# Two transformer blocks on one core: late row factors, the convolution on VectorE, and row-form projections with an earlier attention

## The chip, the cores and the metric

The kernel runs on one core of one Trainium2 chip, in one launch. The metric is the device time of that launch in microseconds (us), the median of several runs. The engines are called TensorE (PE in the profile; PEld is its weight load), VectorE (DVE), ScalarE (ACT), GpSimd (POOL) and SyncE (SP, which issues nearly all DMAs here).

## The reference

256 tokens of width 1024 in float32 pass through two blocks, one layer each.

```python
# first block
h = rmsnorm(x, norm1_g);  z = h @ w_in + b_in          # q k v c_a c_b g_a g_b
br_a = neighbourhood_attention(q, k, v, rpb) @ w_na_out
u = dwconv31(c_a * sigmoid(c_b))                       # 512 channels, 31 taps along the tokens
br_b = silu(layernorm(u)) @ w_conv_out
x = x + (sigmoid(g_a) * br_a + sigmoid(g_b) * br_b) @ w_out
up = dwconv3(rmsnorm(x, norm2_g) @ w_up)               # 2 x 2816 channels
x = x + (gelu(gate) * val) @ w_down                    # gate, val: the halves of up
x = rmsnorm(x, norm_f_g)
# second block
aq, ak, av, mq, mk, mv, mi, mf, mo, ga, gm = split(rmsnorm(x, norm1_gain) @ w_in_2)
att_b = sliding_window_attention(rope(rmsnorm(aq)), rope(rmsnorm(ak)), av, sinks) @ w_branch_attn
hm = rmsnorm(mlstm(mq, mk, mv, mi, mf)) * sigmoid(mo)
mixed = sigmoid(ga) * att_b + sigmoid(gm) * (hm @ w_branch_mlstm)
x = x + mixed @ w_out_2
x = x + peer_ffn(rmsnorm(x, norm2_gain))               # 16 of 16384 experts for each of 8 heads
```

## The kernel before

Every matmul is carried out in the reduced format fp32r as three products, so that it comes out near float32: an operand is split into a high part (rounded to fp32r) and a low part (the rest), and high by high, low by high and high by low are added up. Weights come in **granules** of 128 x 1024 (512 KB): `granule` (L199) has SP load one into one of four `raw` buffers, ScalarE copies out its high part `wh` (L214), and VectorE subtracts to get its low part `wl` (L215; GpSimd for the first two). There are three buffers for each part. A granule is used in one of two forms. `mm_cols` (L233) holds weights stationary and moves 256 columns, all the tokens: 24 matmuls a granule, output with channels on the partitions. `mm_rows` (L243) holds 128 tokens stationary and moves 512 columns of weights: 12 matmuls a granule, output with tokens on the partitions. `turn` (L315) transposes four squares of 128 x 128 into a bank of PSUM and splits them to get a column form. PSUM has four banks "mm" and four "at".

The emitted code says which instructions there are and who needs what; a scheduler sets each engine's order from it, and that order is then fixed. `drive` (L149) interleaves generators by weight: a stream of weight 4 gets four steps where one of weight 1 gets one.

**First block** (L327). The normalized rows are scaled by row factor and gain (`scaled_cols`, L296) and turned. `stream1` (L401) projects c_b and c_a of half the channels (`glu(2)`, which ends with the product `up`, L396), then q, k and v. `stream2` does `glu(0)` and the gates. Beside them run the convolution and the attention. Of the 31 taps of the convolution, half the channels are done on VectorE (L433, L441), half by a product on ScalarE (L445) and an addition on GpSimd (L446). `rows_out` (L653) is the output projection: it computes the new rows `xn`, their squares, the row factor (`power`, L272, on GpSimd), scales by factor and gain (L303) and turns the result for the FFN (L319). The FFN runs over 22 steps `f`: two granules up, the 3-tap convolution, GELU, one granule `down` into four accumulating banks. At its end the last rows are scaled and turned in the same way for the second block.

**Second block** (L725). `stream1` runs alone: akv, the gates' product (`wif`, L788), aq, mq, mk, mv. Then `drive` interleaves `stream2` (mo, ga2, gm2, in column form), the attention at weight 4 and the mLSTM at weight 2. The attention starts with `qk_norm` (L893): for each half i of the tokens ScalarE squares, VectorE sums, takes a reciprocal root by Newton steps (`rsqrt`, L257) and multiplies by factor and gains (L902, L904, L905), GpSimd rotates (L910 to L915, eight instructions), and TensorE transposes q and k (L922, L927, L929). The mLSTM starts with `gates` (L828), a long chain of small VectorE instructions on 8 partitions. The two branch projections ba and bm (column form), the output projection and the experts follow. The experts take the second half of the span and are not touched.

Of the kernel before, what the change touches and what calls it, by code (L numbers as in the profile page):

```python
# [51 lines left out]
def _col(v):  # L52
# [4 lines left out]
         ("cb", 4), ("lg", 4), ("lb", 4), ("fw", 132), ("fb", 44), ("mg", 8), ("gb", 1))  # L57
_ROWS = (("n1", D), ("n2", D), ("nf", D), ("m1", D), ("m2", D), ("b_v", 512), ("qg", 64), ("kg", 64),
# [20 lines left out]
def pack(inputs):  # L79
# [13 lines left out]
        _blocks_b(w2[:, 1792:2304]), _blocks_a(w2[:, 2304:3328], 512), _blocks_b(w2[:, 3344:4368]),  # L93
        _blocks_b(w2[:, 4368:5392]), _blocks_b(w2[:, 5392:6416]), _blocks_b(a["w_branch_attn_2"][0]),
        _blocks_b(a["w_branch_mlstm_2"][0]), _blocks_a(a["w_out_2"][0], 512),
# [16 lines left out]
        _col(a["ffn_dw_b"][0]), _col(a["ml_out_norm_gain_2"][0]), gb], axis=1)  # L112
    rows = np.concatenate([
        a["norm1_g"][0], a["norm2_g"][0], a["norm_f_g"], a["norm1_gain_2"][0], a["norm2_gain_2"][0],
        bi[1024:1536], a["q_norm_gain_2"][0], a["k_norm_gain_2"][0], a["attn_sinks_2"][0]])
# [33 lines left out]
def drive(*gens):  # L149

    live = [[0.0, w, g] for w, g in gens]
    while live:
        e = min(live, key=lambda s: s[0])
        try:
            step = next(e[2])
            e[0] += (step or 1.0) / e[1]
        except StopIteration:
            live.remove(e)


class Block:
# [71 lines left out]
    def mm_cols(self, out, w, x, nk, first=True, last=True, off=0):  # L233

        wh, wl = (t[:, off:off + nk * P].rearrange("p (k n) -> p k n", n=P) for t in w)
        xh, xl = x
        mm = self.nc.tensor.matmul
        for k in range(nk):
            mm(out, wh[:, k], xh[:, k], start=(first and k == 0), stop=False)  # L239
            mm(out, wh[:, k], xl[:, k], start=False, stop=False)  # L240
            mm(out, wl[:, k], xh[:, k], start=False, stop=(last and k == nk - 1))  # L241
# [63 lines left out]

    def warm(self, n):
# [20 lines left out]
def first_block(B, rp):  # L327
    tc, nc, A = B.tc, B.nc, B.A
    with ExitStack() as es:
# [71 lines left out]
        def stream1():  # L401
            yield from glu(2)
            for name, dst, bn in (("q", qT, "b_q"), ("k", kT, "b_k")):
                for n in range(0, 4, 2):
                    b = pair(name, n)
                    for j in range(2):
                        nc.vector.tensor_scalar(dst[:, n + j], b[:, j * T:(j + 1) * T], B.col(bn, n + j), None,
                                                op0=OP.add)
# [11 lines left out]
        def stream2():  # L420
            yield from glu(0)
# [8 lines left out]
        def taps(c0, engines):  # L430
            for c, e in enumerate(engines, c0):
                if e == "D":
                    nc.vector.tensor_scalar(y[:, c], up[:, c, 0:T], B.col("cw", 31 * c), B.col("cb", c), op0=OP.mult,  # L433
                                            op1=OP.add)
                else:
                    nc.scalar.activation(y[:, c], up[:, c, 0:T], AF.Identity, scale=B.col("cw", 31 * c),
                                         bias=B.col("cb", c))
            for k in range(1, 31):
                for c, e in enumerate(engines, c0):
                    if e == "D":  # L440
                        nc.vector.scalar_tensor_tensor(y[:, c], up[:, c, k:k + T], B.col("cw", 31 * c + k), y[:, c],  # L441
                                                       op0=OP.mult, op1=OP.add)
                    else:
                        t = pool.tile([P, T], F32, tag="tap", name="tap", bufs=16)
                        nc.scalar.activation(t, up[:, c, k:k + T], AF.Copy, scale=B.col("cw", 31 * c + k))  # L445
                        nc.gpsimd.tensor_tensor(y[:, c], y[:, c], t, op=OP.add)  # L446
                if k % 3 == 0:
                    yield

        def conv2():  # L450
            while "up2" not in state:
                yield 0.25
            yield from taps(2, "DP")

        def conv():
            while "up0" not in state:
                yield 0.25
            yield from taps(0, "DP")
# [36 lines left out]
        def attention():  # L495
            O = (pool.tile([P, 4, T], FR, name="oh"), pool.tile([P, 4, T], FR, name="ol"))
            for c in range(4):
# [3 lines left out]
                for par in range(2):  # L501
# [24 lines left out]
                    nc.vector.tensor_copy(t, pt.rearrange("p (k q) -> p k q", k=2))  # L526
# [13 lines left out]
        drive((1.0, stream1()), (0.7, conv2()))  # L540
# [4 lines left out]
        drive((1.0, stream2()), (1.3, conv()), (2.0, attention()))  # L545
# [21 lines left out]
        g2 = B.gain(rp, "n2", "gain")  # L567
        X = B.xcol()
        x1 = rows_out(B, rp, "wo", M, x0, 0.5, g2, X, pool,
                      ("qT", "kT", "v", "y", "th", "sig", "oh", "ol"))  # L570


    with ExitStack() as es:
# [3 lines left out]
        late = []  # L577
        acc = [B.bank("at") for _ in range(4)]
# [9 lines left out]

        for f in range(NFF):
            b = B.bank("mm")  # L590
            for j in range(2):
                B.mm_cols(b[:, j * T:(j + 1) * T], B.sec("ffn", 3 * f + j), X, 8)
            u = pool.tile([P, 2, T + 2], F32, tag="u", name="u", bufs=2)
            nc.gpsimd.memset(u[:, :, 0:T + 2:T + 1], 0.0)
            nc.scalar.activation(u[:, :, 1:T + 1], b.rearrange("p (a t) -> p a t", a=2), AF.Copy)
            c = pool.tile([P, 2, T], F32, tag="c", name="c", bufs=2)
            for j in range(2):
                ch = f + NFF * j
                w3 = [B.col("fw", 3 * ch + k) for k in range(3)]
                nc.scalar.activation(c[:, j], b[:, j * T:(j + 1) * T], AF.Identity, scale=w3[1], bias=B.col("fb", ch))  # L600
# [16 lines left out]
        g3 = B.gain(rp, "m1", "gain")  # L617
        gf = B.row_bcast(pool, "nf")
# [696 lines left out]
```

## Time and profile before

| | |
|---|---|
| time, median of 3 runs | 1455.04 us (1454.49 to 1455.75) |
| time of the profiled execution | 1454.76 us |
| its span, first to last instruction | 1453.0 us |
| mean granted TensorE clock | 0.997 |
| busy: TensorE, VectorE, ScalarE, GpSimd | 98%, 75%, 52%, 8% |
| bytes by DMA | 251.44 MB, mean 173 GB/s |

The span is that of one profiled execution; its own time is 1.76 us longer than its span. Busy shares are averages over stages with different limits. A time in a row is the start of an instruction in microseconds from the start of the span, followed by how long it took. A busy TensorE is not one at its peak: matmuls overlap, so their pace is read from one start to the next.

### The profile page before, as it was taken

The page shows a single profiled execution, that of the slowest core. Times are in us where ns is not written, and L with a number is a line of the kernel's source. Part 1 is how long each engine was busy: PE and PEld are TensorE (multiplying, and loading weights), DVE is VectorE, ACT ScalarE, POOL GpSimd, SP SyncE. Part 2 cuts the span into 40 slices and gives each one's busy share as a digit, 9 for nine tenths or more (in the row PEclk, how much of TensorE's full clock was granted, in tenths as well). Part 3 has the DMA queues.
Part 4 walks back from the last instruction along what each step waited for, and adds up shares of the span by engine and source line. Part 5 has one row for each costly group of instructions (what it writes and reads, how often), then busy time and mean ns, then how long its engine had stood idle before and what let it go on. Part 6 is the DMA issues. An engine that isn't in the chain of part 4 may idle for free.

```text
span 1453.0 us, 26393 instructions
## 1 busy us (share of the span) xinstructions
PE 1429.1 (98%) x10351; PEld 1297.6 (89%) x10351; DVE 1092.5 (75%) x1971; ACT 761.2 (52%) x1185; POOL 110.2 (8%) x157
## 2 busy tenths in 40 slices
PE   8899999999999999999999999999999999999998
PEld 7778989999888988988999999999998888888887
DVE  6988876777787567674997976877849999666665
ACT  7476656656564666554454444344444444445443
POOL 4543000000204000001000000000000000000000
PEclk9999999999999999999999999999999999999999
DMA  7534656666466433475455565555565555666663
GB/s 266 168 115 133 180 193 180 187 188 215 135 184 207 144 95 117 145 240 152 148 173 178 170 189 174 161 162 167 167 207 171 172 175 163 189 201 189 192 198 130
DMA packets 70110, 251.44 MB, mean 173 GB/s; under 512 B 8025, under 2 KB 8417, under 8 KB 69730
## 3 DMA queue, kind: packets, MB, share of 16 engines
q1 hardware_dynamic: 69698, 249.17, 55.0%
q8 instruction: 81, 1.33, 0.4%
q10 hardware_dynamic: 288, 0.59, 0.2%
q14 instruction: 43, 0.35, 0.1%
HBM read 247.63 MB, written 2.11 MB: 172 GB/s over the span
## 4 chain that ended last, share of the span: by engine, by line
PE 89%; DVE 7%; issue 1%; ACT 1%; DMA 1%; POOL 1%; SPq 0%; POOLq 0%; ACTq 0%
PE mm L239 16%; PE mm L240 16%; PE mm L241 16%; PE mm L1258 8%; PE mm L1260 8%; PE mm L1259 8%; PE at L1236 2%; PE mm L253 2%; DVE wl L215 2%; PE mm L254 2%; PE mm L252 2%; DVE y L441 2%; PE at L585 1%; PE at L586 1%; PE at L587 1%
## 5 line engine op out<-in xcount | busy, mean ns | idle before, releaser
L215 DVE TENSOR_TENSOR wl<-raw,wh 128x1024 fp32r<-128x1024 f32 x454 | 558.1, 1232 | 202.9 <-ACT wh L214 197.0
L214 ACT ACTIVATE wh<-raw 128x1024 fp32r<-128x1024 f32 (+1 forms) x457 | 479.9, 1052 | 405.6 <-PE mm L240 322.0
L241 PE MATMUL mm<-xh,wl 128*128 128x256 f32 x1952 | 556.3, 285 | 5.6 <-DVE wl L215 5.6
L239 PE MATMUL mm<-xh,wh 128*128 128x256 f32 x1952 | 559.7, 287 | 0.9 <-ACT xh L225 0.9
L240 PE MATMUL mm<-xl,wh 128*128 128x256 f32 x1952 | 557.0, 285 | 0.1
L241 PEld LDWEIGHTS mm<-xh,wl 128*128 128x128 f32 x1952 | 376.2, 193 | 8.7 <-DVE wl L215 6.8
L239 PEld LDWEIGHTS mm<-xh,wh 128*128 128x128 f32 x1952 | 376.0, 193 | 7.1 <-issue 2.9
L240 PEld LDWEIGHTS mm<-xl,wh 128*128 128x128 f32 x1952 | 376.4, 193 | 4.6 <-issue 3.3
L1258 PE MATMUL mm<-wh,wsh 128*128 128x512 f32 x512 | 201.8, 394 | 0.0
L1260 PE MATMUL mm<-wh,wsl 128*128 128x512 f32 x512 | 199.7, 390 | 0.0
L1259 PE MATMUL mm<-wl,wsh 128*128 128x512 f32 x512 | 199.4, 390 | 0.0
L225 ACT ACTIVATE wsh<-W 128x256 fp32r<-128x256 f32 x128 | 53.4, 418 | 188.9 <-PE mm L1259 188.5
L1260 PEld LDWEIGHTS mm<-wh,wsl 128*128 128x128 f32 x512 | 96.2, 188 | 20.3
L1259 PEld LDWEIGHTS mm<-wl,wsh 128*128 128x128 f32 x512 | 96.3, 188 | 19.2
L1258 PEld LDWEIGHTS mm<-wh,wsh 128*128 128x128 f32 x512 | 96.2, 188 | 18.9
L226 DVE TENSOR_TENSOR wsl<-W,wsh 128x256 fp32r<-128x256 f32 x128 | 54.1, 424 | 50.0 <-ACT wsh L225 49.9
L446 POOL TENSOR_TENSOR y<-y,tap 128x256 f32<-128x256 f32 x60 | 58.1, 969 | 52.3 <-ACT tap L445 48.3
L253 PE MATMUL mm<-wl,xh 128*128 128x512 f32 (+1 forms) x160 | 61.1, 382 | 0.6 <-DVE wl L215 0.6
L254 PE MATMUL mm<-wh,xl 128*128 128x512 f32 (+1 forms) x160 | 61.1, 382 | 0.2 <-DVE xl L226 0.2
L252 PE MATMUL mm<-wh,xh 128*128 128x512 f32 (+1 forms) x160 | 61.1, 382 | 0.0
L1239 DVE SCALAR_TENSOR_TENSOR W<-at,W 128x512 f32<-128x512 f32 x64 | 42.7, 686 | 22.5 <-PE at L1236 22.3
L1230 DVE TENSOR_TENSOR bh<-eq,parts 128x512 f16<-128x512 f16 x128 | 48.8, 418 | 0.0
(342 smaller groups left out, 1578.5 us busy)
## 6 DMA issues: line engine op xcount, KB each, us to landing
raw<-in_ws_dram SPq DMA_DIRECT2D x199, 512.0 KB, 3.6
raw<-in_pd_dram SPq DMA_DIRECT2D x128, 512.0 KB, 3.6
raw<-in_pu_dram SPq DMA_DIRECT2D x128, 512.0 KB, 3.6
bias<-in_rpb_dram SPq DMA_DIRECT2D x2, 1024.0 KB, 7.6
x<-in_x_dram SPq DMA_DIRECT2D x4, 256.0 KB, 3.5
r_m<-in_rows_dram SPq DMA_DIRECT2D x2, 512.0 KB, 3.7
mb<-negm_d SPq DMA_DIRECT2D x4, 256.0 KB, 5.1
x<-xn SPq DMA_DIRECT2D x2, 512.0 KB, 5.6
```

Source lines behind the costliest of these rows:

```text
L214: nc.scalar.activation(wh[:, c], raw[:, c], AF.Copy)
L215: eng.tensor_sub(wl[:, c], raw[:, c], wh[:, c].bitcast(F32))
L239: mm(out, wh[:, k], xh[:, k], start=(first and k == 0), stop=False)
L240: mm(out, wh[:, k], xl[:, k], start=False, stop=False)
L241: mm(out, wl[:, k], xh[:, k], start=False, stop=(last and k == nk - 1))
L252: mm(outs[i], xh[:, k0 + k, ts], wh[:, k], start=st, stop=False)
L253: mm(outs[i], xh[:, k0 + k, ts], wl[:, k], start=False, stop=False)
L254: mm(outs[i], xl[:, k0 + k, ts], wh[:, k], start=False, stop=en)
L446: nc.gpsimd.tensor_tensor(y[:, c], y[:, c], t, op=OP.add)
L1258: nc.tensor.matmul(a, wp[0][:, ts], u[0][:, ns], start=(i == 0), stop=False)
L1259: nc.tensor.matmul(a, wp[0][:, ts], u[1][:, ns], start=False, stop=False)
L1260: nc.tensor.matmul(a, wp[1][:, ts], u[0][:, ns], start=False, stop=(i == NE - 1))
```

## The change

It has four parts. (1) At two steps, the entry of the FFN and the entry of the second block, rows are no longer multiplied by their factor before they are turned: only the gain is applied (`plain_cols`), and the factor is applied to the product, on rows as a per-partition scale and on columns by a factor that is spread over the partitions with two small matmuls (`across`). The FFN's input has a buffer of its own, and the first three f's do the first half of K before the second. (2) All taps of the convolution run on VectorE, two channel groups at a time; copies of q, k and the attention weights go to ScalarE; both `glu` come first. (3) In the second block mo, ga2, gm2, ba and bm are done by rows, and the mixed rows are turned afterwards. (4) The second block's `stream1` ends after aq; mq, mk and mv go to `stream2`, so that attention and mLSTM (weights 1.9 and 1.5) are interleaved with them.

```diff
+    def plain_cols(self, pool, src, g, x, k0, i, width=512):
+        for c in range(0, 512, width):
+            ns = slice(k0 * P + c, k0 * P + c + width)
+            y = pool.tile([P, width], F32, tag="nrm", name="nrm", bufs=4)
+            self.nc.vector.tensor_tensor(y, src[:, ns], g[:, ns], op=OP.mult)
+            self.turn(y, x, k0 + c // P, width // P, i)
+
+    def across(self, pool, rp, r, tag):
+        w = rp.tile([P, 2, P], F32, tag="nrm", name="rw", bufs=4)
+        for i in range(2):
+            nc.vector.tensor_copy(w[:, i:i + 1], bc(r[i], P))
+        b = self.bank("at")
+        for i in range(2):
+            nc.tensor.matmul(b[:, i * P:(i + 1) * P], w[:, i], self.ident, start=True, stop=True)
+        rb = pool.tile([P, T], F32, tag=tag, name="rb")
+        nc.scalar.activation(rb, b[:, 0:T], AF.Copy, scale=32.0)
+        return rb
...
+        def taps(c0):
...
             for k in range(1, 31):
-                for c, e in enumerate(engines, c0):
...
+                for c in cs:
+                    nc.vector.scalar_tensor_tensor(y[:, c], up[:, c, k:k + T], B.col("cw", 31 * c + k), y[:, c],
+                                                   op0=OP.mult, op1=OP.add)
+                if k % 2 == 0:
                     yield
...
-        drive((1.0, stream1()), (0.7, conv2()))
+        cv = conv()
+        lead((1.0, stream1()), (1.6, cv))
...
-        drive((1.0, stream2()), (1.3, conv()), (2.0, attention()))
+        drive((1.0, stream2()), (2.0, cv), (1.8, attention()))
...
+        ups = {}
+        ahead = [B.sec("ffn", 3 * f) for f in range(3)]
+        for kh in range(2):
+            for f, w in enumerate(ahead):
+                if f not in ups:
+                    ups[f] = B.bank("mm")
+                B.mm_cols(ups[f][:, 0:T], w, X, 4, kh == 0, kh == 1, kh * 512, 4 * kh)
...
-            nc.scalar.activation(u[:, :, 1:T + 1], b.rearrange("p (a t) -> p a t", a=2), AF.Copy)
+            nc.vector.tensor_tensor(u[:, :, 1:T + 1], b.rearrange("p (a t) -> p a t", a=2), bc_at(rb, 1, 2),
+                                    op=OP.mult)
...
+    if late:
+        return out, r
...
+        def stream2():
             for name, dst in (("mq", mq), ("mk", mk)):
                 for n in range(0, 4, 2):
                     b = pair(name, n)
-                    nc.scalar.activation(dst[:, n:n + 2], b.rearrange("p (a t) -> p a t", a=2), AF.Copy)
+                    nc.vector.tensor_tensor(dst[:, n:n + 2], b.rearrange("p (a t) -> p a t", a=2),
+                                            bc_at(st["rb"], 1, 2), op=OP.mult)
                     yield
...
             for name, dst in (("mo", so), ("ga2", ta), ("gm2", tb)):
-                for n in range(0, 8, 2):
-                    b = pair(name, n)
...
+                for nh in range(2):
...
+                        B.mm_rows(bs, B.sec(name, 4 * nh + gi), X, 2 * gi, 2, 512, gi == 0, gi == 3)
...
-        drive((1.0, stream2()), (4.0, attention()), (2.0, mlstm()))
+        drive((1.0, stream2()), (1.9, attention()), (1.5, mlstm()))
...
+        def second(i, nh, ns, b):
+            t = tb[:, i, ns]
+            nc.vector.scalar_tensor_tensor(t, t, 1.0, b, op0=OP.add, op1=OP.mult)
+            nc.vector.tensor_tensor(t, t, pa[:, i, ns], op=OP.add)
+            B.turn(t, Y, 4 * nh, 4, i)
```

`lead` interleaves like `drive`, but returns when its first generator ends.

The scheduler's order of VectorE's instructions at the start of the convolution, before (`y` on L433 and L441 are the taps, L407 copies q, L396 is `up`):

```order
L396 SCALAR_TENSOR_TENSOR up<-mm,cols,sig 128x256 x2
L433 TENSOR_SCALAR y<-up,cols 128x256
L215 TENSOR_TENSOR wl<-raw,wh 128x1024
L441 SCALAR_TENSOR_TENSOR y<-up,cols,y 128x256 x6
L215 TENSOR_TENSOR wl<-raw,wh 128x1024
L407 TENSOR_SCALAR qT<-mm,cols 128x256 x2
L441 SCALAR_TENSOR_TENSOR y<-up,cols,y 128x256
L215 TENSOR_TENSOR wl<-raw,wh 128x1024
```

and now (taps on L474 and L478, low parts on L231, `up` on L435):

```order
L435 SCALAR_TENSOR_TENSOR up<-mm,cols,sig 128x256 x2
L474 TENSOR_SCALAR y<-up,cols 128x256 x2
L478 SCALAR_TENSOR_TENSOR y<-up,cols,y 128x256 x16
L432 TENSOR_SCALAR sig<-sig 128x512
L231 TENSOR_TENSOR wl<-raw,wh 128x1024 x2
L478 SCALAR_TENSOR_TENSOR y<-up,cols,y 128x256 x4
L231 TENSOR_TENSOR wl<-raw,wh 128x1024 x2
```

Eighteen taps now stand between `up` and the next low part, where one stood.

TensorE's order where q and k of the first half of the tokens are transposed (L922 to L929), before, in the midst of the projection mo:

```order
L240 MATMUL mm<-xl,wh 128x256
L241 MATMUL mm<-xh,wl 128x256
L922 MATMUL at<-ident,qk 128x128 x8
L927 MATMUL at<-ident,qk 128x128
L929 MATMUL at<-ident,ks 128x128
L239 MATMUL mm<-xh,wh 128x256
```

and now (L996 to L1003), after all of mq and four matmuls of mk; L255 to L257 are the three products of `mm_cols`, L958 transposes a row of the gates:

```order
L257 MATMUL mm<-xh,wl 128x256
L255 MATMUL mm<-xh,wh 128x256
L256 MATMUL mm<-xl,wh 128x256
L255 MATMUL mm<-xh,wh 128x256
L256 MATMUL mm<-xl,wh 128x256
L996 MATMUL at<-ident,qk 128x128 x8
L1001 MATMUL at<-ident,qk 128x128
L1003 MATMUL at<-ident,ks 128x128
L958 MATMUL at<-ident,fi 128x8 x2
```

Before, mq, mk, mv and two granules of mo came ahead of these transposes; now only mq and the start of mk do. The second half's transposes now stand 33 matmuls behind the transposes of `mt` (L958), two matmuls before the end of mk.

VectorE's order around the row that releases the rotation of the first half, before (L902 to L905 are the products of `qk_norm`, L267 and L268 Newton steps, L858 the gates' scan):

```order
L902 TENSOR_TENSOR qk<-qk,rsy 128x1152
L215 TENSOR_TENSOR wl<-raw,wh 128x1024
L904 TENSOR_TENSOR qk<-qk,qg 128x1024
L905 TENSOR_TENSOR qk<-qk,qg 128x128
L267 SCALAR_TENSOR_TENSOR rst<-rsy 128x18
L215 TENSOR_TENSOR wl<-raw,wh 128x1024
L268 TENSOR_TENSOR rst<-rst,ss 128x18
```

and now (L976 to L979; L874 takes mq out of PSUM and multiplies it by the spread factor):

```order
L976 TENSOR_TENSOR qk<-qk,rsy 128x1152
L932 COPY gz_4742<-gz 8x2x4
L974 TENSOR_SCALAR ss<-ss 128x18
L978 TENSOR_TENSOR qk<-qk,qg 128x1024
L979 TENSOR_TENSOR qk<-qk,qg 128x128
L874 TENSOR_TENSOR mq<-mm,rb 128x512
L931 TENSOR_TENSOR gz<-gz_4742 8x2x120
L932 COPY gz<-gz_4742 8x2x8
L280 TENSOR_SCALAR rsy<-ss 128x18
L231 TENSOR_TENSOR wl<-raw,wh 128x1024
```

The row of mq, which waits for the last matmul of mq, now stands between the release of the rotation and the next low parts.

## Rows read from the trace of the kernel before

Times are in us from the start of the span; a line of `...` marks rows left out.

**Rows 1.** The page, part 1: busy time, share of the span, instructions.

```profile
PE 1429.1 (98%) x10351; PEld 1297.6 (89%) x10351; DVE 1092.5 (75%) x1971; ACT 761.2 (52%) x1185; POOL 110.2 (8%) x157
```

**Rows 2.** Windows: window, its length, engines' busy us (instructions), PEclk, DMA share, GB/s.

```profile
50.00:75.00 25.00, 23.17 (x127) 20.24 (x128) 22.48 (x30) 8.12 (x9) 7.16 (x8) 0.93 0.56 174
200.00:225.00 25.00, 24.61 (x194) 24.07 (x195) 19.63 (x43) 19.05 (x32) 0.31 (x3) 1.00 0.43 138
425.00:450.00 25.00, 25.00 (x202) 24.64 (x201) 24.83 (x68) 14.06 (x20) 8.46 (x6) 1.00 0.55 179
650.00:675.00 25.00, 22.05 (x150) 20.42 (x149) 11.38 (x19) 9.15 (x16) 4.53 (x4) 0.93 0.50 160
```

**Rows 3.** TensorE's waits: engine, line, releaser, us in total, times, longest us.

```profile
PE mm L241 <- DVE wl L215: 5.6, 6, 2.0
...
PE mm L253 <- DVE wl L215: 0.6, 1, 0.6
```

**Rows 4.** TensorE's timeline: start, us, line, out<-in, form. Second block aq, transposes, experts' query.

```profile
415.16 0.39 PE L253 MATMUL mm<-wl,xh 128*128 128x512 f32 x1
...
417.88 0.39 PE L253 MATMUL mm<-wl,xh 128*128 128x512 f32 x1
...
475.71 1.03 PE L922 MATMUL at<-ident,qk 128*128 128x128 f32 x8
...
849.92 0.28 PE L239 MATMUL mm<-xh,wh 128*128 128x256 f32 x1
...
850.28 0.28 PE L239 MATMUL mm<-xh,wh 128*128 128x256 f32 x1
```

**Rows 5.** TensorE's timeline, single waits: in brackets the idle time before and its releaser.

```profile
46.01 0.39 PE L241 MATMUL mm<-xh,wl 128*128 128x256 f32 x1 [1.98 <-DVE wl L215]
...
51.18 0.39 PE L241 MATMUL mm<-xh,wl 128*128 128x256 f32 x1 [2.04 <-DVE wl L215]
...
199.48 0.44 PE L319 MATMUL at<-ident,nrm 128*128 128x128 f32 x2 [2.20 <-DVE nrm L303]
...
390.19 1.32 PE L319 MATMUL at<-ident,nrm 128*128 128x128 f32 x8 [0.76 <-DVE nrm L303]
...
396.25 0.44 PE L319 MATMUL at<-ident,nrm 128*128 128x128 f32 x2 [1.45 <-DVE nrm L303]
...
658.00 0.44 PE L319 MATMUL at<-ident,nrm 128*128 128x128 f32 x2 [2.37 <-DVE nrm L303]
```

**Rows 6.** VectorE's timeline, beside the convolution with GpSimd idle.

```profile
59.05 0.47 DVE L441 SCALAR_TENSOR_TENSOR y<-up,cols,y 128x256 f32<-128x256 f32 x1
59.44 0.86 DVE L407 TENSOR_SCALAR kT<-mm,cols 128x256 f32<-128x256 f32 x2
...
60.62 1.21 DVE L215 TENSOR_TENSOR wl<-raw,wh 128x1024 fp32r<-128x1024 f32 x1
```

**Rows 7.** Groups of VectorE's instructions from 25 to 130 us: busy us, mean ns, idle before.

```profile
L441 DVE SCALAR_TENSOR_TENSOR y<-up,cols,y 128x256 f32<-128x256 f32 x60 | 43.3, 721 | 1.3
L215 DVE TENSOR_TENSOR wl<-raw,wh 128x1024 fp32r<-128x1024 f32 x27 | 37.0, 1378 | 2.1 <-ACT wh L214 2.1
```

**Rows 8.** GpSimd's timeline, rotation of q and k, first and second half.

```profile
441.46 1.46 POOL L910 TENSOR_TENSOR rt<-qk,cos 128x144 f32<-128x144 f32 x1 [42.70 <-DVE rst L267]
...
443.36 4.44 POOL L910 TENSOR_TENSOR rt<-qk,cos 128x144 f32<-128x144 f32 x1
...
450.78 0.54 POOL L910 TENSOR_TENSOR rt<-qk,cos 128x144 f32<-128x144 f32 x1
...
457.46 0.24 POOL L915 COPY ks<-qk 128x64 f32<-128x64 f32 x1
```

**Rows 9.** TensorE's first matmul after the gates' product; VectorE's products with the gains.

```profile
403.33 0.40 PE L252 MATMUL mm<-wh,xh 128*128 128x512 f32 x1
...
441.04 0.27 DVE L905 TENSOR_TENSOR qk<-qk,qg 128x128 f32<-128x128 f32 x1
...
446.03 1.21 DVE L904 TENSOR_TENSOR qk<-qk,qg 128x1024 f32<-128x1024 f32 x1
```

More of the change, by code (lines that the diff above doesn't have):

```diff
@@ L157, in drive, with lead @@
         except StopIteration:
+            live.remove(e)
+def lead(main, *others):
+    live = [[0.0, w, g] for w, g in (main,) + others]
+    first = live[0]
+    while True:
+        e = min(live, key=lambda s: s[0])
+        try:
+            step = next(e[2])
+            e[0] += (step or 1.0) / e[1]
+        except StopIteration:
+            if e is first:
+                return
             live.remove(e)
@@ L231, in xcol, with mm_cols @@
         return h, l
-    def mm_cols(self, out, w, x, nk, first=True, last=True, off=0):
+    def mm_cols(self, out, w, x, nk, first=True, last=True, off=0, k0=0):
         wh, wl = (t[:, off:off + nk * P].rearrange("p (k n) -> p k n", n=P) for t in w)
@@ L238, in mm_cols @@
         for k in range(nk):
-            mm(out, wh[:, k], xh[:, k], start=(first and k == 0), stop=False)
-            mm(out, wh[:, k], xl[:, k], start=False, stop=False)
-            mm(out, wl[:, k], xh[:, k], start=False, stop=(last and k == nk - 1))
+            mm(out, wh[:, k], xh[:, k0 + k], start=(first and k == 0), stop=False)
+            mm(out, wh[:, k], xl[:, k0 + k], start=False, stop=False)
+            mm(out, wl[:, k], xh[:, k0 + k], start=False, stop=(last and k == nk - 1))
     def mm_rows(self, outs, w, x, k0, nk, width, first, last, off=0, tiles=(0, 1)):
@@ L428, in stream2 @@
                     yield
-        def taps(c0, engines):
-            for c, e in enumerate(engines, c0):
[L432 to L437, printed above, removed]
-            for k in range(1, 31):
[L439 to L447, printed above, removed]
+        def taps(c0):
+            while "up%d" % c0 not in state:
+                yield 0.25
+            cs = (c0, c0 + 1)
+            for c in cs:
+                nc.vector.tensor_scalar(y[:, c], up[:, c, 0:T], B.col("cw", 31 * c), B.col("cb", c), op0=OP.mult,
+                                        op1=OP.add)
+            for k in range(1, 31):
+                for c in cs:
+                    nc.vector.scalar_tensor_tensor(y[:, c], up[:, c, k:k + T], B.col("cw", 31 * c + k), y[:, c],
+                                                   op0=OP.mult, op1=OP.add)
+                if k % 2 == 0:
                     yield
[L450 to L453, printed above, removed]
         def conv():
-            while "up0" not in state:
-                yield 0.25
-            yield from taps(0, "DP")
+            yield from taps(2)
+            yield from taps(0)
             with B.tc.high_priority():
@@ L566, in first_block @@
         B.show("mergedx2", tb)
[L567 to L570, printed above, removed]
+        g2 = B.row_bcast(rp, "n2", tag="gain")
+        X = tuple(fp.tile([P, 8, T], FR, name="xf" + c) for c in "hl")
+        x1, r1 = rows_out(B, rp, "wo", M, x0, 0.5, g2, X, pool,
+                          ("qT", "kT", "v", "y", "th", "sig", "oh", "ol"), late=True)
     with ExitStack() as es:
@@ L746, in second_block @@
                                 channel_multiplier=-1)
-        hg = pool.tile([P, 8], F32, name="hg")
-        nc.vector.tensor_scalar(hg, B.col("mg", 0, 8), 0.5, None, op0=OP.mult)
+        hg = B.row_bcast(rp, "mg", tag="gain")
+        nc.gpsimd.tensor_scalar(hg, hg, 0.5, None, op0=OP.mult)
+        rr = pool.tile([P, 2, 2], F32, name="rr")
+        for i in range(2):
+            nc.gpsimd.tensor_scalar(rr[:, 0, i:i + 1], r3[i], 32.0, None, op0=OP.mult)
+            nc.gpsimd.tensor_scalar(rr[:, 1, i:i + 1], r3[i], 16.0, None, op0=OP.mult)
+        full = [rr[:, 0, i:i + 1] for i in range(2)]
+        half = [rr[:, 1, i:i + 1] for i in range(2)]
         qk = pool.tile([P, 2, 18, 64], F32, name="qk")
@@ L991, in mlstm @@
             yield from gates()
+            while "mv" not in st:
+                yield 0.25
             aT, em = st["aT"], st["em"]
@@ new lines, in branch, with first @@
+        def branch(name, x, done):
+            for nh in range(2):
+                bs = [B.bank("mm"), B.bank("mm")]
+                for gi in range(4):
+                    B.mm_rows(bs, B.sec(name, 4 * nh + gi), x, 2 * gi, 2, 512, gi == 0, gi == 3)
+                for i in range(2):
+                    done(i, nh, slice(nh * 512, nh * 512 + 512), bs[i])
+        def first(i, nh, ns, b):
+            nc.vector.scalar_tensor_tensor(pa[:, i, ns], ta[:, i, ns], 1.0, b, op0=OP.add, op1=OP.mult)
@@ L1081, in second_block @@
+        branch("bm", M, second)
         B.show("mixedx2", tb)
```

155 lines of the change are left out of this document (79 added, 76 removed).

## The prediction, made before the changed kernel had run

> **What bounds the kernel now.** The first view is the page's share of busy time: TensorE is busy for 98% of the span, VectorE for 75% [rows 1]. So a microsecond counts only where TensorE has fewer matmuls, or waits more or less than before. The second view is the windows with the granted clock: it stands at 1.00, except at 0.93 in two stretches of 25 us [rows 2]. A mean of 0.93 is 3.5 us at the lower of the two levels (1.2 for 2.4 GHz), so each dip takes about 1.7 us. The third is TensorE's waits by releaser and the single waits in the timeline [rows 3, 5]. The two 2-us waits at 46 and 51 us came before the first dip, the one of 2.37 us before 658.00 ahead of the second; after the wait of 2.20 us that ended at 199.48 the window from 200 to 225 us reads 1.00. A wait of some 2.2 us is therefore at the edge of being paid twice, and a longer one is likely to be.
>
> **1. Form of 40 granules** (mo, ga2, gm2, ba, bm: eight each). By columns one granule is 24 matmuls of 256 columns; three of these take 850.28 − 849.92 = 0.36 us, so 0.12 each and 2.88 us a granule. By rows it is 12 matmuls of 512 columns, and twelve in aq lie 417.88 − 415.16 = 2.72 us apart [rows 4]. Saved: 40 × 0.16 = 6.4 us. Added on TensorE are 16 transposes that turn the mixed rows and 4 small matmuls that spread the factors; at 1.03 us for eight [rows 4] that is 20 × 0.13 = 2.6. **Net −3.8.** The work is on TensorE in both kernels, so nothing hides it.
>
> **2. Convolution on VectorE.** Before, TensorE waited 5.6 + 0.6 us for low parts of weights [rows 3], nearly all of it beside the convolution, where VectorE's 60 taps averaged 721 ns and its 27 low parts 1378 ns [rows 7]; with GpSimd idle they take 0.47 (0.39 from one start to the next) and 1.21 [rows 6]. Now there are 120 taps, all on VectorE, and no GpSimd additions: 120 × 0.39 = 47 us in place of 43, and the low parts give back 27 × 0.17 = 4.6. The copies of q, k and the attention weights go to ScalarE. VectorE has less to do in all, so I let the old waits go, 6.2, and the dip behind them, 1.7. But the first piece of the new order puts 18 taps between the two rows `up` and the next low part: with `up` and the twice as wide `sig` 22 × 0.39 = 8.6, and 1.2 for the low part itself. TensorE has two granules in hand then, 5.8 us, and reaches the low part 0.2 later: a wait of 9.8 − 6.0 = 3.8. Its bounds: 0 if the scheduler's granules are further ahead, 5.5 if the clock dips behind it. **Net −4.1.**
>
> **3. Entry and exit of the FFN.** At the entry the product with the gain no longer needs the row factor, so it follows the new rows at once; the wait of 2.20 us [rows 5] goes, but TensorE now meets the two spreading matmuls, which need the second factor, 11 matmuls later. I leave 0.9 there. **−1.3.** At the exit the waits of 0.76 and 1.45 us [rows 5] go: 28 matmuls of the last f's and of akv stand between the last transposes and the spreading. **−2.2.** Late here is the second factor's column for ScalarE, behind a wide product on GpSimd's queue; only copies of akv wait for it, which nothing needs for 20 us. The 22 products with the spread factor move from ScalarE to VectorE, at 0.7 us in every 8.6 (three granules); VectorE is busy for 19.6 of 25 us there [rows 2], so it still has room. If that cover were gone TensorE would wait for low parts again, as in part 2. Three more loads of rows of 4 KB on SP's queue are free as long as four raw buffers are ahead of the matmuls.
>
> **4. Attention sooner: first transposes of q and k.** Before, they came at 475.71 us, 18 us after GpSimd had ended the rotation at 457.70 [rows 4, 8]. In the new order they stand 84 matmuls of 512 and 100 of 256 columns behind the gates' product: 84 × 0.2265 + 100 × 0.12 = 31.0 us. When can they run? Before, L905, the row that releases the rotation of the first half, ended 441.31 − 403.33 = 38.0 us after that product [rows 9]. The new order puts 8 low parts ahead of it in place of 11 (−3.5), less of the second half (−1.4), and does the first half of mq on VectorE (+0.7), which makes 33.8; some of VectorE's short waits should close up, and I take 32.5. Then GpSimd's eight rows. Before, they took 9.3 us for the first half and 6.9 for the second; rows of the same shape took 0.54 or 4.44 us [rows 8]. Undisturbed, six at 0.5 and two copies are 3.5. Beside two low parts the second half took 6.9; the new order has two there also, with smaller rows around, and I take 5.5. The transposes run at 32.5 + 5.5 = 38.0: **a wait of 7.0**, with 5.0 and 10.8 as ends by 3.5 and 9.3. Behind them on TensorE stands all of mk.
>
> Why a row of 0.54 becomes one of 4.44 is not said by the rows, only that wide VectorE rows ran beside it: the product with the gains, 1.21 us from 446.03, lies inside it [rows 8, 9]. The Trainium skill, SBUF — State Buffer, section "SBUF: two separate sides", calls the pair of ports that VectorE and GpSimd share an exclusive lock that is held for a whole instruction, so that each of the eight could wait for a whole low part. By that rule the wait would be 14 us and the sum 1468; the trace agrees that GpSimd is the one that loses, but its undisturbed rows beside the narrow gate rows speak for less.
>
> **5. Second transposes.** TensorE transposes `mt`, VectorE copies it (0.2), then comes the second half's product with the gains (1.2 and 0.3) [rows 9], GpSimd's eight rows (5.5), and TensorE has only 33 matmuls, 4.0 us, until it wants them: 7.2 − 4.0 = **3.2**, ends 1.2 and 4.6 (by 3.5 and 6.9). Both waits are above those that came before a dip, so I add **two dips, 3.4**. The ends are one less and, for the wait in part 2, one more.
>
> **6. The rest.** Attention and mLSTM now run under mv to gm2; in two places their VectorE rows between two low parts come to 8 and 10 us, an estimate at 0.3 to 0.7 us a row, against three buffers of 2.72 us: **+1.0** (0 to 3). The turn of the mixed rows before the last projection waits for its last two VectorE rows: **+0.7** (0 to 2.2, the entry's wait).
>
> **Sum.** −3.8 − 4.1 − 1.3 − 2.2 = −11.4; 7.0 + 3.2 + 3.4 + 1.0 + 0.7 = +15.3; together +3.9 on the profiled execution's 1454.76 us, which lies 0.3 under the median of the three runs: **1458.7 us**. Its own range: with 3.5 us of rotation 2.0 + 2.0 less and a dip less, 1453.0; with 9.3 and 6.9, 3.8 + 1.4 more and a third dip, 1465.6.
>
> **Rivals.** *The rotation is in time.* If VectorE reaches the releasing row some 6 us sooner (its part before 32.5 us holds waits for ScalarE that could close), neither wait nor dip comes, the gains stand and the rest costs 1.7: 1454.8 − 11.4 + 1.7 = **1445.1**. For it speaks that the rows are short (about 0.2 to 0.7 us); against it, that VectorE was busy for 24.83 of the 25 us from 425 [rows 2]. *The rotation is held up by every low part* (part 4): eight rows of GpSimd at 0.5, six to eight of them behind 1.2 us, make 12.7; 7.2 more at the first place and 2.4 at the second: **1468.3**, slower. It decides from the point where more than two low parts run while the rotation does; TensorE's wait itself speaks against it, as VectorE's low parts soon have no free buffer. *The convolution's start costs nothing or the waits there stay*: ±4 around the forecast, inside its range. That the form saves nothing could be if matmuls of 512 columns ran slower in the branches: up to 3.8 more, also inside.
>
> **Chances.** About what can be told from no change is 0.2%, 2.9 us, so 1452.1 to 1457.9. The forecast has 0.52: 0.02 faster, 0.21 same, 0.29 slower. In time: 0.26, nearly all faster (0.25 and 0.01). Held up: 0.10, slower. One of the two waits only, about 1452: 0.12 (0.05, 0.06, 0.01). Together 0.32, 0.28, 0.40. The range reaches from the rival in time to just short of the one held up, 1445 to 1467; half of the one, most of the other, and a little of the rest fall outside.
>
> **What will show it.** In TensorE's waits: L319's entry is down to the norm at the start and the one at 658 us; one wait of 3 to 4 us for a low part near 31 us and hardly any later beside the convolution; two waits at the transposes of q and k, on GpSimd, of 7 and 3 us, near 430 and 445 us; matmuls of mo at 0.2265 us. In GpSimd's rows the rotation at 5 to 6 us a half. Wrong would be: no wait over 1 us at L996, a rotation of over 9 us, or waits for low parts that add up to more than before.

## The result

The changed kernel took **1463.48 us** (median of 5 runs, 1461.05 to 1463.98) against 1455.04 (5 runs): **slower by 0.52%** (ratio 1.0052, 95% interval 1.0041 to 1.0063). The profiled execution took 1462.46 us, 7.7 more than that of before. The page's busy times of after:

```profile
PE 1430.7 (98%) x9895; PEld 1275.9 (87%) x9895; DVE 1103.8 (76%) x2030; ACT 734.8 (50%) x1117; POOL 60.3 (4%) x106
```

GpSimd's share has halved, VectorE's and TensorE's are as in [rows 1]. Which stage lost the time is read from TensorE's timeline, at four places that both kernels have: the first projection matmul, the first of the output projection, the gates' product, and the last turn before the experts. Before:

```profile
11.02 0.58 PE L239 MATMUL mm<-xh,wh 128*128 128x256 f32 x1
...
174.18 0.39 PE L252 MATMUL mm<-wh,xh 128*128 128x512 f32 x1
...
400.53 0.28 PE L788 MATMUL mm<-xh,wifh 128*40 128x256 f32 x1
...
661.84 0.42 PE L319 MATMUL at<-ident,nrm 128*128 128x128 f32 x1
```

and after:

```profile
11.65 0.58 PE L255 MATMUL mm<-xh,wh 128*128 128x256 f32 x1
...
168.94 0.39 PE L268 MATMUL mm<-wh,xh 128*128 128x512 f32 x1
...
399.33 0.36 PE L854 MATMUL mm<-xh,wifh 128*40 128x256 f32 x1
...
669.66 0.41 PE L356 MATMUL at<-ident,nrm 128*128 128x128 f32 x1
```

One granule of aq (2.72 us) stands ahead of the gates' product now and stood behind it before; it is put back in this table.

| stage | before | after | measured | forecast |
|---|---|---|---|---|
| up to the first projection | 11.02 | 11.65 | +0.6 | 0 |
| projections, convolution, attention | 163.16 | 157.29 | −5.9 | −4.1 |
| output projection, FFN | 226.35 | 230.39 − 2.72 | +1.3 | −3.0 |
| second block up to the experts | 261.31 | 270.33 + 2.72 | +11.7 | +11.0 |
| experts | 791.2 | 791.0 | −0.1 | 0 |

The forecast's column sorts the prediction's terms by stage; the four spreading matmuls (0.5 of the 2.6 us in part 1) stand in the FFN's. TensorE's waits of after, by releaser, and the largest one by one:

```profile
PE at L996 <- POOL qk L986: 8.5, 2, 5.4
...
PE at L356 <- DVE nrm L327: 4.4, 6, 1.1
PE mm L257 <- DVE wl L231: 2.6, 2, 2.1
```

```profile
34.81 0.38 PE L257 MATMUL mm<-xh,wl 128*128 128x256 f32 x1 [2.13 <-DVE wl L231]
...
183.18 0.66 PE L356 MATMUL at<-ident,nrm 128*128 128x128 f32 x4 [1.07 <-DVE nrm L327]
...
383.65 0.66 PE L356 MATMUL at<-ident,nrm 128*128 128x128 f32 x4 [1.02 <-DVE nrm L327]
...
389.84 0.41 PE L356 MATMUL at<-ident,nrm 128*128 128x128 f32 x2 [0.87 <-DVE nrm L327]
...
391.16 0.44 PE L356 MATMUL at<-ident,nrm 128*128 128x128 f32 x2 [0.79 <-DVE nrm L327]
...
434.00 0.39 PE L255 MATMUL mm<-xh,wh 128*128 128x256 f32 x1 [0.79 <-ACT wh L230]
...
439.93 1.97 PE L996 MATMUL at<-ident,qk 128*128 128x128 f32 x8 [5.43 <-POOL qk L986]
...
458.58 1.81 PE L996 MATMUL at<-ident,qk 128*128 128x128 f32 x8 [3.10 <-POOL qk L986]
```

The two waits for the rotation are there, 5.43 and 3.10 us, with one of 0.79 just ahead, and the waits for low parts beside the convolution are down to one place near 34 us (before, 6.2 in all [rows 3]). After three of them, those that ended at 34.81, 439.93 and 458.58, the clock fell:

```profile
25.00:50.00 25.00, 22.08 (x170) 21.68 (x169) 22.91 (x46) 8.88 (x11) 0.00 (x0) 0.93 0.65 229
425.00:450.00 25.00, 18.78 (x133) 17.87 (x132) 18.98 (x55) 7.41 (x11) 6.25 (x8) 0.86 0.35 107
450.00:475.00 25.00, 21.90 (x129) 17.65 (x128) 15.50 (x30) 11.53 (x29) 5.09 (x8) 0.93 0.48 157
```

Before, the stretches from 425 and 450 us stood at 1.00 (the first in [rows 2]). A mean of 0.93 is some 3.4 us at the lower level with matmuls running, 1.7 us lost. A mean of 0.86 is 6.8 us at that level, but the first 1.6 of them lie in the wait itself, where TensorE has nothing to do: the level falls at 438.3, the wait ends at 439.93, and the level is back at 445.1. So about 2.6 us are lost there, 4.3 with the second stretch:

```profile
440.00:445.00 5.00, 5.00 (x23) 4.64 (x24) 1.89 (x8) 1.47 (x3) 0.35 (x2) 0.50 0.53 173
445.00:450.00 5.00, 5.00 (x41) 4.85 (x40) 2.08 (x5) 1.68 (x2) 0.00 (x0) 0.99 0.06 11
```

What TensorE waited for at 439.93 is seen in the rows of VectorE and GpSimd:

```profile
433.54 0.27 DVE L979 TENSOR_TENSOR qk<-qk,qg 128x128 f32<-128x128 f32 x1
...
433.96 0.49 POOL L984 TENSOR_TENSOR rt<-qk,cos 128x144 f32<-128x144 f32 x1 [33.59 <-ACT wh L230]
434.41 1.96 POOL L984 TENSOR_TENSOR rt<-qk,sin 128x144 f32<-128x144 f32 x1
436.33 1.93 POOL L984 TENSOR_TENSOR rt<-qk,cos 128x144 f32<-128x144 f32 x1
...
439.34 0.53 POOL L986 TENSOR_TENSOR qk<-rt 128x144 f32<-128x144 f32 x1
```

```profile
434.81 1.20 DVE L231 TENSOR_TENSOR wl<-raw,wh 128x1024 fp32r<-128x1024 f32 x1
...
436.70 1.21 DVE L231 TENSOR_TENSOR wl<-raw,wh 128x1024 fp32r<-128x1024 f32 x1
```

The row that releases the rotation ends at 433.81, the last row that the transposes wait for at 439.87: 6.1 us, of which two rows of 1.9 are the held-up ones (before, one of 4.44 [rows 8]). Each of the two has one of VectorE's low parts within it, and ends some 0.35 us after that low part.

### The profile page after: what moved, and what is told of

It is laid out like the page before. It is cut to its first block, busy times and chain, and to the rows that moved or that the text cites. A ratio compares the mean times of both kernels' runs of the same rounds, so it can differ in the third digit from the quotient of the medians.

```text
span 1460.7 us, 25361 instructions
## 1 busy us (share of the span) xinstructions
PE 1430.7 (98%) x9895; PEld 1275.9 (87%) x9895; DVE 1103.8 (76%) x2030; ACT 734.8 (50%) x1117; POOL 60.3 (4%) x106
## 4 chain that ended last, share of the span: by engine, by line
PE 90%; DVE 6%; issue 1%; DMA 1%; ACT 1%; POOL 1%; SPq 0%; ACTq 0%; DVEq 0%; POOLq 0%
PE mm L255 14%; PE mm L257 14%; PE mm L256 14%; PE mm L1332 8%; PE mm L1334 8%; PE mm L1333 8%; PE mm L268 5%; PE mm L269 5%; PE mm L270 4%; PE at L1310 2%; DVE wl L231 2%; PE at L617 1%; PE at L618 1%; PE at L619 1%; DMA raw<-in_ws_dram 1%
## 5 line engine op out<-in xcount | busy, mean ns | idle before, releaser
L231 DVE TENSOR_TENSOR wl<-raw,wh 128x1024 fp32r<-128x1024 f32 x454 | 553.7, 1222 | 188.9 <-ACT wh L230 186.0
L255 PE MATMUL mm<-xh,wh 128*128 128x256 f32 x1408 | 404.4, 287 | 2.1 <-ACT wh L230 1.6
L257 PE MATMUL mm<-xh,wl 128*128 128x256 f32 x1408 | 400.9, 285 | 2.6 <-DVE wl L231 2.6
L256 PE MATMUL mm<-xl,wh 128*128 128x256 f32 x1408 | 401.8, 285 | 0.0
L255 PEld LDWEIGHTS mm<-xh,wh 128*128 128x128 f32 x1408 | 272.1, 193 | 5.4 <-ACT wh L230 2.3
L257 PEld LDWEIGHTS mm<-xh,wl 128*128 128x128 f32 x1408 | 272.3, 193 | 3.8 <-DVE wl L231 3.0
L256 PEld LDWEIGHTS mm<-xl,wh 128*128 128x128 f32 x1408 | 272.4, 193 | 2.1 <-issue 1.8
L268 PE MATMUL mm<-wh,xh 128*128 128x512 f32 (+1 forms) x256 | 100.4, 393 | 0.0
L255 PE MATMUL mm<-xfh,wh 128*128 128x256 f32 x352 | 100.2, 285 | 0.0
L269 PE MATMUL mm<-wl,xh 128*128 128x512 f32 (+1 forms) x256 | 100.1, 391 | 0.0
L257 PE MATMUL mm<-xfh,wl 128*128 128x256 f32 x352 | 100.0, 284 | 0.0
L256 PE MATMUL mm<-xfl,wh 128*128 128x256 f32 x352 | 99.1, 282 | 0.0
```

Of the source, the lines that this page charges most:

```text
L231: eng.tensor_sub(wl[:, c], raw[:, c], wh[:, c].bitcast(F32))
L255: mm(out, wh[:, k], xh[:, k0 + k], start=(first and k == 0), stop=False)
L256: mm(out, wh[:, k], xl[:, k0 + k], start=False, stop=False)
L257: mm(out, wl[:, k], xh[:, k0 + k], start=False, stop=(last and k == nk - 1))
L268: mm(outs[i], xh[:, k0 + k, ts], wh[:, k], start=st, stop=False)
L269: mm(outs[i], xh[:, k0 + k, ts], wl[:, k], start=False, stop=False)
```

## The experiments

Eleven kernels ran; times are medians, beside runs of the kernel before on the same chip.

**1. Attention later.** Part 4 undone in the changed kernel:

```diff
-        def stream2():
             for name, dst in (("mq", mq), ("mk", mk)):
...
+        def stream2():
             for name, dst in (("mo", so), ("ga2", ta), ("gm2", tb)):
...
-        drive((1.0, stream2()), (1.9, attention()), (1.5, mlstm()))
+        drive((1.0, stream2()), (4.0, attention()), (2.0, mlstm()))
```

> The changed kernel with its fourth part undone: mq, mk and mv are again projected in stream1, attention and mLSTM have weights 4 and 2; TensorE's transposes of q and k move back some 210 matmuls. Theory (the two waits on GpSimd's rotation, 5.4 and 3.1 us, the wait of 0.8 for a granule beside them, and the lower clock behind them, 0.86 and 0.93 in two stretches of 25 us, 5.2 us): all of it goes, 1463.5 - 14.5 = 1449 us (1447 to 1452), no wait at L997. Rival (the second block is longer because its row form is slower beside attention, whatever the order): the waits go but the time is found again under mo to gm2, over 1457 us.

Measured 1451.9 us (1450.17 to 1454.92), 0.9979 of before (0.9969 to 0.9988). No wait at the transposes is left and the clock stays up:

```profile
425.00:450.00 25.00, 25.00 (x186) 23.89 (x185) 25.00 (x60) 9.57 (x11) 5.79 (x9) 1.00 0.56 170
450.00:475.00 25.00, 24.81 (x115) 20.32 (x114) 14.59 (x17) 12.56 (x16) 6.28 (x8) 1.00 0.74 232
```

So by the two ratios 10.6 us hang on the place of the transposes (with the weights of the streams, which go back with it). It was to be 14.5. That took 5.2 us for the clock, which cost 4.3, and the low part of the branch projection ba now comes 2.5 us late (L269); in the profiled execution the clock stays at 1.00 behind that wait.

**2. The product with the final gain on VectorE.** At the FFN's exit, in the changed kernel:

```diff
-                nc.gpsimd.tensor_tensor(y, t, gf[:, ns], op=OP.mult)
+                nc.vector.tensor_tensor(y, t, gf[:, ns], op=OP.mult)
```

> The changed kernel with the product with the final gain at the FFN's exit on VectorE in place of GpSimd, four instructions. Theory (GpSimd's four products, 1.5 to 1.8 us each, hold up VectorE's products with the next gain, two of which took 2.99 in place of 1.37 us, and with them the transposes): the waits at L356 behind L327 at the exit, 3.3 us, fall to 1.5 or less, 1463.5 - 2.5 = 1461 us (1460 to 1462). Rival (VectorE is the bound there itself; it gets 2.7 us more work): no change or slower, 1463 to 1466.

The kernel before had only the first of these four products on GpSimd; the change had put the other three there, too:

```diff
-                (nc.vector if hf or i else nc.gpsimd).tensor_tensor(y, t, gf[:, ns], op=OP.mult)
+                nc.gpsimd.tensor_tensor(y, t, gf[:, ns], op=OP.mult)
```

Measured 1460.87 us (1456.97 to 1463.37), 1.0035 of before (1.0024 to 1.0045). That is 2.6 less than the changed kernel, as the first theory has it, but the two intervals overlap; runs 1 and 3, which differ by the same edit, are clear of each other. In the changed kernel VectorE's two products with the next gain take 2.99 us beside GpSimd's, and even a row of 128 x 1 takes 1.23. The first fence is GpSimd's and VectorE's timeline there, the second VectorE's in this run:

```profile
380.08 2.97 POOL L680 TENSOR_TENSOR y<-x,r_nf 128x512 f32<-128x512 f32 x2 [16.92 <-DVE x L677]
...
380.61 2.99 DVE L327 TENSOR_TENSOR nrm<-x,r_m 128x512 f32<-128x512 f32 x2
...
387.40 1.23 DVE L686 SCALAR_TENSOR_TENSOR u<-v,u 128x1 f32<-128x1 f32 x1
...
389.27 1.83 DVE L327 TENSOR_TENSOR nrm<-x,r_m 128x256 f32<-128x256 f32 x2
```

```profile
382.59 0.68 DVE L327 TENSOR_TENSOR nrm<-x,r_m 128x512 f32<-128x512 f32 x1
...
383.79 0.69 DVE L327 TENSOR_TENSOR nrm<-x,r_m 128x512 f32<-128x512 f32 x1
...
389.58 0.75 DVE L327 TENSOR_TENSOR nrm<-x,r_m 128x256 f32<-128x256 f32 x2
```

VectorE does four instructions more and is ready sooner; the waits at the exit for the product with the gain are gone from TensorE's list. The one at the FFN's entry, which the edit does not touch, rose from 1.07 to 2.13 us in the profiled execution, with 0.93 in the stretch from 175 us; no run says why, and it takes back some of the gain.

**3. Both.** 

> Both edits of the two runs before. Theory: the effects add up, 1449 - 2.5 = 1446.5 us (1444 to 1450), below the kernel before by 0.6%. Rival (one wait stands for the other): no better than the better of the two by over 1 us.

Measured 1446.79 us (1446.46 to 1448.88), 0.9946 (0.9929 to 0.9962). The kernel is faster than before. By the ratios it gains 15.4 us on the changed kernel, where the two edits alone gave 10.6 and 2.5: neither wait stood for the other, and the sum is at least reached.

**4. The rotation on VectorE**, the transposes where the changed kernel has them: eight instructions from `nc.gpsimd` to `nc.vector`.

> The changed kernel with the rotation of q and k, eight instructions a half, on VectorE in place of GpSimd; the transposes stay where they are in TensorE's order. Theory (the rotation itself, 6.4 and 5.2 us on GpSimd beside VectorE's rows, is what TensorE waits for): it takes about 2 us a half, the waits at L996 fall from 8.5 us to 1 to 3, one dip of the clock goes, 1463.5 - 8 = 1455.5 us (1453 to 1458). Rival (the place in the order is the cost: VectorE then brings the low parts of mk later, and TensorE waits for those): waits of L257 for low parts appear, 1459 to 1464 us.

Measured 1454.52 us (1451.16 to 1457.63), 0.9996 (0.9986 to 1.0005). On VectorE a rotation row takes 0.29 us, and TensorE's waits there are

```profile
435.86 1.07 PE L996 MATMUL at<-ident,qk 128*128 128x128 f32 x8 [1.64 <-issue]
...
437.77 0.39 PE L257 MATMUL mm<-xh,wl 128*128 128x256 f32 x1 [0.41 <-DVE wl L231]
```

The 1.64 us that are left, put down to "issue", end with VectorE's last rotation row before the transposes:

```profile
435.46 0.29 DVE L986 TENSOR_TENSOR qk<-rt 128x144 f32<-128x144 f32 x1
```

So of the 10.6 us that run 1 ties to the place, 8.1 (by the ratios) come because GpSimd's rotation lies between VectorE's row and the transposes. The rival's wait for a low part is there too, but with 0.41 us.

**5. Part 4 alone**, on the kernel before: the edit of run 1 the other way round.

> The kernel before with the fourth part of the change alone: mq, mk and mv move to stream2, attention and mLSTM have weights 1.9 and 1.5; everything else as before. The transposes of q and k now stand behind all of mq and half of mk's first granules. Theory (the place of the transposes is what makes the change slower): two waits at L924 on GpSimd of some 5 and 3 us and one or two dips of the clock, 1455.8 + 11 = 1467 us (1463 to 1471). Rival (the waits come only from the late factors, which put further VectorE rows ahead of the rotation): no wait over 1 us there, 1454 to 1458.

Measured **1475.31 us** (1474.54 to 1476.14), 1.014 (1.0123 to 1.0156): the theory's sign and place, at nearly twice its size. The first wait for the rotation is 2 us longer than expected, the second as expected. The clock stands lower too, at 0.83 and 0.82 in the two stretches; together that is 17 us at the lower level. Of these 6.2 lie in the waits, where TensorE has nothing to do (the third row is most of the first wait), so some 5.4 us are lost:

```profile
446.83 1.97 PE L924 MATMUL at<-ident,qk 128*128 128x128 f32 x8 [7.15 <-POOL qk L914]
...
463.11 1.11 PE L924 MATMUL at<-ident,qk 128*128 128x128 f32 x4 [3.43 <-POOL qk L914]
```

```profile
425.00:450.00 25.00, 17.85 (x126) 17.14 (x126) 22.65 (x73) 11.73 (x18) 7.22 (x8) 0.83 0.49 158
450.00:475.00 25.00, 21.57 (x134) 19.96 (x133) 12.14 (x20) 9.33 (x18) 5.18 (x8) 0.82 0.34 113
...
441.50:446.75 5.25, 0.00 (x0) 0.00 (x0) 5.25 (x14) 0.00 (x0) 5.17 (x6) 0.52 0.61 197
```

The rest came at the branch bm, where the mLSTM's rows were late by 1.9 and 1.3 us (0.7 before), and with further stretches at the lower clock, one of them (200 to 225 us at 0.88) ahead of the edit.

**6. Part 2 alone**, on the kernel before (its hunks of the diff). 

> The kernel before with the second part alone: all taps on VectorE, copies of q, k and attention weights on ScalarE, both glu first. Theory (the changed kernel's first stage came 5.9 us shorter in the two traces): 1455.8 - 5.9 = 1450 us (1448 to 1452), one wait of 2 us and one of 0.8 at 34 us and none later beside the convolution. Rival (part of that gain came from the FFN's entry, which starts the projections' end earlier): 1452 to 1455.

Measured 1450.26 us (1447.9 to 1451.86), 0.9968 (0.9955 to 0.998): the theory, 1 us short.

**7. Part 3 alone.** 

> The kernel before with the third part alone: mo, ga2, gm2, ba, bm by rows. Theory (40 granules at 2.72 in place of 2.88 us, 16 transposes more): 1455.8 - 4.3 = 1451.5 us (1450 to 1453.5). Rival (rows beside attention run slower, 0.23 us a matmul and more, or a low part in ba comes late by 2.6 us as in the runs with attention later): 1453.5 to 1456.5.

Measured 1455.65 us (1454.35 to 1457.7), 1.0004 (0.9995 to 1.0014): **no gain**, the rival's second half. Twelve matmuls of 512 columns in mo, from 480.20 us, take 2.72 as forecast; but the branch projection ba waits for its first low part, and the clock falls behind it:

```profile
590.53 0.50 PE L254 MATMUL mm<-wl,oh 128*128 128x512 f32 x1 [2.99 <-DVE wl L216]
```

```profile
575.00:600.00 25.00, 22.01 (x104) 16.32 (x102) 19.24 (x59) 15.52 (x38) 0.00 (x0) 0.93 0.38 127
```

That is 2.99 + 1.7 us. The form saves less: in this stage a granule by rows takes 2.75 us on the average (28 of them without a break) and took 2.85 by columns in the kernel before (26), so 40 granules save 4.0, and the 16 transposes take back about 2. The profiled execution, at 1457.59, is one of the slowest of the ten. What VectorE does before that low part are wide rows of the mLSTM's norm, with rows of the softmax between them:

```profile
586.33 1.21 DVE L1046 TENSOR_TENSOR hn<-num,den 128x1024 f32<-128x1024 f32 x1
...
588.06 1.21 DVE L1048 TENSOR_TENSOR hn<-hn,so 128x1024 f32<-128x1024 f32 x1
```

**8. Parts 2 and 3.** 

> The kernel before with parts two and three, so without late factors and without the earlier attention. If the parts add up: 1455.8 - 5.9 - 4.3 = 1445.6 us (1443 to 1449). Theory (the late factors are worth about nothing as they are, and 2 us with the product on VectorE): within 2 us of the run with both edits, 1446.8. Rival (late factors are worth their 3.5 us): 1449 to 1452.

Measured 1449.45 us (1448.04 to 1450.9), 0.9964 (0.9951 to 0.9976). That is what runs 6 and 7 make together (0.9972), but 4 us more than the sum that was expected of the parts, and 2.7 us above run 3, where the theory allowed 2: the number fell into the rival's range. Against this run, late factors are worth 2.6 us with the product on VectorE (run 3, by the ratios) and cost 2.2 as the change has them (run 1). In both pairs the intervals overlap, so what late factors are worth stays open.

**9. The convolution's start.** Run 3 with the convolution at weight 1.0 beside the first stream; ten taps stand ahead of the next low part:

```diff
-        lead((1.0, stream1()), (1.6, cv))
+        lead((1.0, stream1()), (1.0, cv))
```

> The version with attention later and the product on VectorE, and the convolution's generator at weight 1.0 in place of 1.6 beside the first stream: about ten taps in place of 18 stand between the first up and the next low part. Theory (the waits of 0.8 and 2.1 us near 31 and 34 us, and the dip of the clock behind them that some executions show, come from that block): both waits go, 1446.8 - 3 = 1443.8 us, less up to 1 where the dip was (1442 to 1445). Rival (the taps come later and the layer norm of the convolution, with its projection, waits): the time stays within 1 us of 1446.8 and a wait of over 1 us appears at the convolution's normalization near 140 us.

Measured 1445.78 us (1444.41 to 1448.72). Both waits at the start went, and three of 0.4 to 0.5 us came where the convolution's result meets its projection (153 us): 1.0 us gained by the medians in place of 3. Each theory had half of it; with intervals of 0.3% the gain itself is not clear.

**10. Attention and mLSTM at weights 6 and 3**, else as run 9. 

> The run before with weights 6 and 3 in place of 4 and 2 for attention and mLSTM beside stream2; the projections mq, mk, mv stay ahead of it. The softmax and norm rows then end before the branch projection ba begins. Theory (the wait of 2.5 us for a low part in ba and the clock's dip behind it come from those rows): the wait goes, 1443.8 - 2.5 = 1441.3 us, a little less without the dip (1439 to 1443). Rival (rows that come sooner delay low parts of ga2 or gm2 by as much): no change within 1 us, the wait in another place.

Measured **1442.51 us** (1441.72 to 1443.43), 0.991 (0.9893 to 0.9926): the lowest median of all, 13.8 us under the 1456.28 of the kernel before on that chip. The theory holds. The wait in ba is gone; of the waits at the transposes of normalized rows are left those at the start and before the experts' query, and one at the FFN's entry:

```profile
PE at L356 <- DVE nrm L319: 3.9, 2, 2.5
...
PE at L356 <- DVE nrm L327: 1.3, 1, 1.3
```

**11. Only mv later**, weights 4 and 2, else as run 9. 

> As the run two before, but with mv (not mq and mk) in stream2: the transposes of q and k stand some 115 matmuls of 256 columns later than in the changed kernel and 96 of 512 columns sooner than with attention later. Theory (attention sooner costs only where TensorE gets to the transposes before the rotation is done; at the changed kernel's pace the rotation ends some 5 us after its place, and the second half's some 3 us): no wait over 1 us for the first half, at most 2 us for the second; no wait in ba; 1441 to 1445 us. Rival (every sooner start costs VectorE's rows in the wrong place): over 1447 us.

Measured 1444.72 us (1443.03 to 1447.46), 0.9925 (0.9908 to 0.9942). With 96 matmuls fewer ahead of the transposes than in run 9, no wait for the rotation is left; one of 1.8 us for a softmax appears. An earlier attention is not slow in itself: the theory holds. The intervals of runs 9, 10 and 11 overlap, so which of them is best is not shown.

## Why the prediction was right, and where it was not

The range held the time and the likeliest case had the sign. Its 1458.7 us lay 4.8 below the median; the median is still inside that case's own range of 1453.0 to 1465.6. On the profiled execution the forecast was +3.9 and +7.7 came. By stages the miss of 3.8 is +0.6, −1.8, +4.3 and +0.7: the FFN's is by far the largest. Step by step:

- **Part 4, first transposes (7.0 forecast).** Right: the wait is 5.43 us, and would have been 6.2 without the 0.79 that TensorE lost on another wait just ahead. The release came 31.6 us after the gates' product (32.5 forecast), the rotation took 6.1 (5.5). Run 4 shows that it is the rotation on GpSimd, run 1 that it is the place.
- **Part 5, second transposes (3.2).** Right: 3.10.
- **Two dips (3.4).** Right in kind, too small: 4.3 in the profiled execution, since the clock stayed down twice as long at the longer wait. In run 5, with a wait of 7.15 us, some 5.4 were lost.
- **Part 1, the form (−3.8).** Mis-sized. I took the pace of columns from the experts' query and that of rows from aq. Between the transposes and the end of bm a granule took 2.85 us by columns before and 2.75 by rows now, so 40 granules save 4.0 us in place of 6.4: −1.4 net. I also left out what stands next: by rows the projections end before VectorE is through with the rows of the mLSTM's norm and the softmax, and ba waits (run 7). In the changed kernel that wait is absent, and it is back where the attention comes later (run 1); the two parts are not independent.
- **Part 2, the convolution (−4.1).** −5.9. The waits in this stage fell from 6.8 to 3.5 us, and the dip that I let go stayed (0.93 from 25 us). So some 2.6 us of the gain lie in the matmuls between the waits, and no run says why. The wait of 3.8 at its start came as 0.79 + 2.13, and taps and low parts are as fast as the rows of before without GpSimd said (0.47 and 1.21 us [rows 6]):

```profile
L478 DVE SCALAR_TENSOR_TENSOR y<-up,cols,y 128x256 f32<-128x256 f32 x120 | 50.2, 472 | 0.0
L231 DVE TENSOR_TENSOR wl<-raw,wh 128x1024 fp32r<-128x1024 f32 x28 | 33.8, 1214 | 2.1 <-ACT wh L230 2.0
```

- **Part 3, the exit of the FFN (−2.2): the step that failed.** "At the exit the waits of 0.76 and 1.45 us go": other waits took their place, 3.3 us in five pieces, at transposes that wait for the product with the gain. The sign that was named, such waits only at the start and at 658 us, failed with it. I had costed the four products on GpSimd at nothing, and for GpSimd's queue had asked only who waits for it; they cost by slowing VectorE's product, on which TensorE waits (run 2; in time, run 3 against run 1). With the entry (−1.2 on its waits, as forecast), the exit (+1.1) and the four matmuls (+0.5) about 1 us of the stage's +1.3 stays open.
- **The rest (+1.7).** It did not come: the form (−1.9 without the spreading matmuls), the three waits (9.3) and the clock (4.3) already make the +11.7 of the second block. That its sum was close to the forecast's +11.0 is luck: the form saved 2.4 us too little and the rest cost 1.7 too little.

The rule that was weighed in part 4, that the shared pair of ports is held for a whole instruction (the Trainium skill, SBUF — State Buffer, "SBUF: two separate sides"), agrees with the rows of 1.9 us in this: each lasted until shortly after the low part beside it, although it is recorded as begun 0.4 us before that. The wait of 14 us that I had worked out by it did not come, because two low parts ran beside the first rotation and not six to eight. At the exit, where the step failed, the rule agrees as well: it lets whichever starts first block the other, and there VectorE's row of 128 x 1 took 1.23 us and ended at 388.63, as GpSimd's product did (386.84 + 1.78). I had read it for GpSimd's side alone. No run here takes the ports apart from other causes.

## What to carry to other kernels

A step moved forward is paid for at the place where its chain crosses engines: count the producer's rows from the release, not the free time of the engine that does them. An instruction put on an idle engine is not free when it slows the engine on the chain beside which it runs, as GpSimd's products slowed VectorE's; here it was cheaper on the chain's own engine. And a stage that is made shorter on TensorE hands its end to whatever VectorE still has queued there, so a saving is to be read together with the next wait.

## What was not expected of the hardware

The lower clock behind a wait is not a fixed price. The waits of 0.8 and 2.1 us near 34 us are the same in runs 1 and 3, but the stretch stands at 0.93 in one profiled execution and at 1.00 in the other:

```profile
25.00:50.00 25.00, 22.07 (x170) 21.66 (x169) 23.33 (x47) 8.76 (x12) 0.00 (x0) 0.93 0.66 229
```

```profile
25.00:50.00 25.00, 22.08 (x182) 21.67 (x181) 24.85 (x50) 9.41 (x12) 0.00 (x0) 1.00 0.66 241
```

The wait of 2.46 or 2.47 us before the experts' query shows it too: behind it the clock stood at the lower level for 3.4 us in the changed kernel, not at all in runs 3 and 9, and for some 7 us in run 10. So a wait of about 2 us costs 1.7 us more in some executions and not in others. The spread of a version from run to run goes with the clock: in run 2 the executions at a mean clock of 0.994 took 1457 to 1459 us, those at 0.990 took 1463. The waits of 5.43 and 7.15 us took the clock down in all the profiled executions that had them, and it fell before they ended. And a GpSimd product over 128 x 512 slows one on VectorE beside it: VectorE's two took 2.99 us, against 0.68 each without it. What GpSimd's two, at 2.97, would take alone no run shows.
